# A 1024x1024 output product taken as seven products of quarters, with the weights' sums made by transfers in DRAM

## The chip, the cores and the metric

The kernel runs on one core of a Trainium2 chip. The metric is the device time of one execution in microseconds (us), as the median of several runs. The engines of the core are TensorE (PE, whose weight loads are listed apart as PEld), VectorE (DVE), ScalarE (ACT), GpSimd (POOL) and SyncE (SP), which here only issues transfers. Each engine takes its instructions from one queue in a fixed order.

## What is computed

Two transformer blocks on 512 tokens of width 1024, all in float32. The change lies in the end of the first block: the merged branches are multiplied by `w_out`.

```python
def first_block(x, p, ...):
    ...
    att_b = fox_branch(qb, kb, vb, log_f)                  # forgetting attention, 8 heads
    y_b = (att_b * silu(gate_b)) @ w_branch_b
    m_a, m_b = split(sigmoid(h @ w_merge))
    out = (m_a * y_a + m_b * y_b) @ w_out                  # [512, 1024] @ [1024, 1024]
    x = x + rmsnorm(out, g_post)
    e = p @ w_ple                                          # [512, 256] @ [256, 1024]
    gate = sigmoid(x @ w_ple_gate)
    x = x + rmsnorm(gate * e, g_ple)
    return x
```

The second block (attention, and a feed-forward part with `w_gate`, `w_up`, `w_down`) follows. The test compares with this reference in float32.

## The kernel before

Every float32 product is three matmuls: a value is split into a rounded part (`wh` of a weight, `ah` of an activation) and its rest (`wl`, `al`), and `wh*ah`, `wl*ah` and `wh*al` are added up in PSUM. A matmul here is 128x128 by 128x512.

Weights come as one stream. `specs` lists the products in the order of their use, `stream` cuts them into groups of 1024 columns (two 128-row chunks of 512 columns each, for the output product), and the stream is walked with a fixed lead: SP's queue loads a group into `raw` up to five groups ahead of use (`load_to`), and `convert_to` makes `wh` by a cast on ACT (L333) and `wl` by a subtraction on DVE (L334), up to three groups ahead. `wh` and `wl` have four buffers each, so the conversion of a group waits until the matmuls of the group four earlier are done. `send` hangs a further transfer behind the conversion of certain groups (`behind`). That is how sums of quarters of the second block's `w_down` come to DRAM: plain copies on SP's queue from the start of the stream on, and later adding transfers on POOL's queue (L249), each behind a one-element-per-partition copy `poke` (L248) that waits for that group's cast.

The feed-forward part at the end already takes `w_down` as a product of quarters with seven instead of eight products. The output product doesn't: it is `out0` and `out1`, two halves of the columns with eight chunks of the inner dimension each. Around it stand, in order of the program:

- the forgetting attention (`fox`), whose softmax scaling runs on POOL (L612 the reciprocal `rr`, L613 `P` times `rr`), whose transposes of `P` run on PE (L651), and into which products of later use are woven;
- `ya0` and `ya1`, whose results, per chunk of 128 columns, are evacuated by DVE (L986, L987) and split on ACT and DVE (L525) into `mh`, `ml`, the activation of the output product. This is transposed: columns on the partitions, tokens along the free dimension;
- the output product, with evacuation by `ev_out` (L1011 times `g_post`, L545 the square sum on ACT, L1014 the addition to `xr`, behind `rstd2` on POOL) and then `to_T`: eight transposes of the new `xr` of one token block on PE (L553), four to a PSUM bank `T`, of which there are two, each bank split into `x2h` (ACT, L521) and `x2l` (DVE, L522);
- `e0` and `e1`, the small product with `w_ple`, and then `pg0`, which reads `x2h` and `x2l`.

The order of these products on each engine is left to a scheduler, which mixes instructions of neighbouring products; inside `ordered()` the order on PE is that of the program instead. A list `late` holds back pieces of work for a number of steps (`LATE`), counted by `tick`.

## Time and profile before

| what | value |
|---|---|
| median of the runs | 1200.07 us (3 runs, 1199.03 to 1200.73) |
| the profiled execution's own time | 1198.17 us |
| its span, first to last instruction | 1196.4 us |
| mean granted clock of TensorE | 0.995 |
| busy: PE, DVE, ACT, POOL | 1166.9, 845.0, 637.9, 292.3 us |

The profile is of one execution. Busy time is the union of an engine's instructions. For PE the ends of matmuls are modelled, and they overlap: the pace of matmuls is read from their starts. An idle time stands in brackets behind an instruction, with the instruction that released it. The granted clock is a share of full speed, which is 2.4 GHz.

### The profile page before, as it was taken

How to read it: one execution, taken by the hardware profiler on the slowest of the kernel's cores; microseconds unless marked ns; L12 is line 12 of the kernel's file. 1: busy time of each engine (PE TensorE's matmuls, PEld its weight loads, DVE VectorE, ACT ScalarE, POOL GpSimd, SP SyncE). 2: the span in 40 equal slices, each digit the busy share in tenths (PEclk: the TensorE clock that was granted, in tenths of full speed). 3: DMA queues.
4: the chain of work that ended last, by engine and by line, in shares of the span. 5: the costliest groups of instructions: out<-in, count | busy, mean ns of one | idle time of the engine just before them, and what ended most of it. 6: DMA issues, size and time to landing. Idle time of an engine off the chain costs nothing.

```text
span 1196.4 us, 18475 instructions
## 1 busy us (share of the span) xinstructions
PE 1166.9 (98%) x6634; PEld 1009.8 (84%) x6634; DVE 845.0 (71%) x1569; ACT 637.9 (53%) x1260; POOL 292.3 (24%) x500
## 2 busy tenths in 40 slices
PE   7999999999999999999999999999999999999997
PEld 5898888888888888879888878888899999998885
DVE  5578767796565753776445478874698887877895
ACT  4466356535663444544466567752555455556564
POOL 2011065403341020211333435410022212200124
PEclk9999999999999999999999999999999999999999
DMA  5423613443223523324222222155369798857553
GB/s 195 102 92 119 191 48 119 126 137 102 95 71 106 181 85 109 127 90 128 57 71 72 72 60 79 60 158 193 124 127 185 147 190 151 141 132 268 170 184 114
DMA packets 117403, 148.89 MB, mean 124 GB/s; under 512 B 15552, under 2 KB 70080, under 8 KB 117312
## 3 DMA queue, kind: packets, MB, share of 16 engines
q1 hardware_dynamic: 94528, 136.18, 36.2%
q0 software_dynamic: 22784, 11.54, 8.2%
q8 instruction: 52, 0.85, 0.3%
q14 instruction: 39, 0.32, 0.1%
HBM read 141.40 MB, written 29.36 MB: 143 GB/s over the span
## 4 chain that ended last, share of the span: by engine, by line
PE 84%; DVE 4%; issue 4%; ACT 3%; POOL 2%; DMA 2%; SPq 0%; POOLq 0%; ACTq 0%; DVEq 0%
PE mm L422 49%; PE mm L1404 7%; PE E L1404 5%; PE R L1404 5%; PE S L1597 4%; PE AV L666 3%; PE E L1597 3%; PE T L651 2%; PE mm L1597 2%; DVE wl L334 1%; ACT wh L333 1%; DMA raw<-in_w_in_dram 1%; PE T L553 1%; PE S L885 1%; PE S L884 1%
## 5 line engine op out<-in xcount | busy, mean ns | idle before, releaser
L334 DVE TENSOR_TENSOR wl<-raw,wh 128x512 fp32r<-128x512 f32 (+4 forms) x219 | 203.2, 945 | 89.3 <-ACT wh L333 88.4
L333 ACT CAST wh<-raw 128x512 fp32r<-128x512 f32 (+4 forms) x219 | 173.7, 815 | 162.2 <-PE mm L422 65.7
L612 POOL TENSOR_TENSOR rr<-rs,mone 128x1 f32<-128x1 f32 x128 | 75.5, 590 | 166.5 <-ACT P L606 106.0
L522 DVE TENSOR_TENSOR pl<-T,ph 128x128 fp32r<-128x128 f32 (+3 forms) x152 | 61.9, 412 | 60.9 <-ACT ph L521 60.2
L422 PE MATMUL mm<-hh,wh 128*128 128x512 f32 x256 | 103.5, 405 | 0.0
L422 PE MATMUL mm<-hl,wh 128*128 128x512 f32 x256 | 101.4, 396 | 0.0
L422 PE MATMUL mm<-hh,wl 128*128 128x512 f32 x256 | 100.5, 395 | 0.0
L606 ACT ACTIVATE P<-P,nm 128x128 f32<-128x128 f32 (+2 forms) x96 | 51.5, 537 | 51.4 <-DVE nm L599 47.4
L521 ACT CAST ph<-T 128x128 fp32r<-128x128 f32 (+3 forms) x152 | 54.7, 362 | 43.5 <-PE T L651 32.1
L613 POOL TENSOR_SCALAR P<-P,rr 128x256 f32<-128x256 f32 (+3 forms) x128 | 73.4, 573 | 12.0
L333 ACT CAST wh<-qsum 128x1024 fp32r<-128x1024 f32 (+1 forms) x44 | 42.8, 974 | 53.9 <-PE R L1404 16.3
L1404 PE MATMUL R<-acts,wh 128*128 128x256 f32 x320 | 57.8, 281 | 0.0
L1404 PE MATMUL mm<-acts,wh 128*128 128x256 f32 x320 | 57.6, 280 | 0.0
L651 PE MATMUL T<-ident,P 128*128 128x128 f32 x296 | 54.3, 277 | 3.3 <-ACT km L1184 2.4
L422 PEld LDWEIGHTS mm<-hh,wl 128*128 128x128 f32 x256 | 48.0, 188 | 11.2
L1404 PE MATMUL E<-acts,wh 128*128 128x256 f32 x320 | 57.1, 280 | 0.0
L334 DVE TENSOR_TENSOR wl<-qsum,wh 128x1024 fp32r<-128x1024 f32 (+1 forms) x44 | 49.3, 1122 | 11.0 <-ACT wh L333 11.0
L422 PEld LDWEIGHTS mm<-hh,wh 128*128 128x128 f32 x256 | 48.2, 188 | 8.5
L422 PEld LDWEIGHTS mm<-hl,wh 128*128 128x128 f32 x256 | 48.2, 188 | 7.8
L422 PE MATMUL mm<-h2h,wh 128*128 128x512 f32 x128 | 53.6, 419 | 0.0
L422 PE MATMUL mm<-h2h,wl 128*128 128x512 f32 x128 | 50.6, 395 | 0.0
L422 PE MATMUL mm<-h2l,wh 128*128 128x512 f32 x128 | 50.1, 392 | 0.0
(431 smaller groups left out, 3458.8 us busy)
## 6 DMA issues: line engine op xcount, KB each, us to landing
raw<-in_w_in_dram SPq DMA_DIRECT2D x50, 512.0 KB, 3.7
down<-in_w_down_dram SPq DMA_DIRECT2D x16, 704.0 KB, 6.0
quart<-in_w_up_dram SPq DMA_DIRECT2D x20, 512.0 KB, 6.4
raw<-down SPq DMA_DIRECT2D x20, 512.0 KB, 3.9
raw<-in_w_merge_dram SPq DMA_DIRECT2D x16, 512.0 KB, 4.1
raw<-in_w_out_dram SPq DMA_DIRECT2D x16, 512.0 KB, 3.9
quart<-in_w_gate_dram SPq DMA_DIRECT2D x16, 512.0 KB, 5.2
raw<-in_w_down_dram SPq DMA_DIRECT2D x15, 512.0 KB, 4.3
```

The source lines that it names most:

```text
L333: mark_hi[0] = nc.scalar.copy(hi[:, js], raw[:, js]).ins
L334: mark[0] = nc.vector.tensor_sub(lo[:, js], raw[:, js], hi[:, js].bitcast(F32)).ins
L422: nc.tensor.matmul(o, x_, m, start=kc == 0 and k == 0 and n0 == 0, stop=last and k == 2)
L521: nc.scalar.copy(hi, src)
L522: nc.vector.tensor_sub(lo, src, hi.bitcast(F32))
L606: nc.scalar.activation(P[:, :n], P[:, :n], AF.Exp, bias=bias, scale=-1.0, accum_out=rs)
L612: nc.gpsimd.tensor_tensor(rr, rs, mone, op=OP.pow)
L613: nc.gpsimd.tensor_scalar(P[:, :n], P[:, :n], rr, 1.0, op0=OP.mult, op1=OP.mult)
L651: nc.tensor.transpose(T[:, i, :], P[:, blk(i)], ident)
L666: nc.tensor.matmul(self.av[:, q0:q0 + pc.stop - pc.start], self.v(kb), m, start=pi == 0 and i == 0, stop=pi == len(plan) - 1 and i == 1)
L1404: nc.tensor.matmul(R[:, c, :], w[:, kc, cs], m[:, kc, :], start=first and c + kc + k == 0, stop=kc == 3 and k == 2, skip_group_check=True)
L1597: nc.tensor.matmul(acc[b], a, w[:, j], start=first and kc == 0 and k == 0, stop=kc == 10 and k == 2, skip_group_check=True)
```

## The change

The output product is made by seven products of quarters (512x512) instead of the eight that two halves amount to: `A11`, `S4`, `A12`, `S2`, `S1`, `S3`, `A22`, each over 4 chunks of the inner dimension for 2 token blocks of 128 and 512 columns, with the three matmuls of the split. So the groups of the weight stream are 14 where they were 8, and everything behind them moves by that. Sums `S1` to `S4` of the weights' quarters are made in DRAM: four copies of 1 MB on SP's queue, behind the conversions of groups 14, 16, 18 and 20, and four adding transfers of 1 MB on POOL's queue behind the conversions of groups 27, 29, 31 and 35. The copies of `w_down`, which began at group 14, begin at 22; its adding transfers keep their places in the feed-forward part. The sums `T1` to `T4` of the activation's quarters are made in place in `ta` by DVE and split like the activation itself.

The results are put together from PSUM banks of three kinds: `S` for `A11`, `mm` and `AV` for `S4`, two `mm` for `U` (a negated copy of `A11` by ACT to which `S2` and `S3` add), and again `S` for `A22`. The whole from `A11` to `e1` stands in one `ordered()` block, and the transposes of `xr` wait eight steps (`LATE["out"]`). The transposes of `p` (`pst`) move ahead into `ya0` and `ya1`.

```diff
-    LATE = {"mla": 3, "pg1": 16, "q2": 8, "o21": 10}
+    LATE = {"mla": 3, "pg1": 16, "q2": 8, "o21": 10, "out": 8}
...
+    in_dram = {}
+    def quarter(base, w, name):
+        n = w.shape[0] // 2
+        if name[0] == "S":
+            if (base, name) not in in_dram:
+                in_dram[base, name] = tc.dram_tile([n, 512], F32, name=f"{base}{name}")
+            return in_dram[base, name]
+        r, c = n * (name[2] == "2"), 512 * (name[1] == "2")
+        return w[r:r + n, c:c + 512]
+    def quarters(base, w, order):
+        return {base + name: ([(quarter(base, w, name), 0, 512, 0)], w.shape[0] // 256) for name in order}
+    OUT = ("A11", "S4", "A12", "S2", "S1", "S3", "A22")
...
-        "out0": ([(w_out, 0, 512, 0)], 8),
-        "out1": ([(w_out, 512, 512, 0)], 8),
+        **quarters("out", w_out, OUT),
...
-        for some, engine, at, step in ((copies, nc.sync, 14, 2), (adds, nc.gpsimd, first_of["seven"], 4)):
+        def put(some, engine, base, w, rows, at):
             for dst, src in some:
-                for r in range(0, DFF // 2, 352):
-                    behind[at] = (engine, down_sums[dst][r:r + 352, :], down(src)[r:r + 352, :])
-                    at += step
+                for r in range(0, w.shape[0] // 2, rows):
+                    behind[at.pop(0)] = [engine] + [quarter(base, w, q)[r:r + rows, :] for q in (dst, src)]
+        put(copies, nc.sync, "out", w_out, 512, [14, 16, 18, 20])
+        put([adds[i] for i in (0, 3, 1, 2)], nc.gpsimd, "out", w_out, 512, [27, 29, 31, 35])
+        put(copies, nc.sync, "dn", w_down_2, 352, list(range(22, 54, 2)))
+        put(adds, nc.gpsimd, "dn", w_down_2, 352, list(range(first_of["seven"], first_of["seven"] + 64, 4)))
...
-    mh, ml = unit("mh", "U3"), unit("ml", "U6")
+    m21 = unit("m21", "U3", [128, 2, 4, 512])
+    m11 = unit("m11", "U6", [128, 2, 2, 4, 256])
+    mT = unit("mT", "U0", [128, 2, 2, 4, 256])
+    m4 = [pool.tile([128, 4, 256], FR, name="m4", tag=f"V{2 + k}") for k in range(2)]
+    mp = {"B11": m11[:, 0], "B22": m21[:, :, :, :256], "B21": m21[:, :, :, 256:], "T1": m11[:, 1],
+          "T2": mT[:, 0], "T3": mT[:, 1]}
+    mp = {**{n: [t[:, 0], t[:, 1]] for n, t in mp.items()}, "T4": m4}
     def ev_ya(g):
         def f(c, ps):
             i = 4 * g + c
             t = p2("ya")
             nc.vector.scalar_tensor_tensor(t, ta[:, i, :], 1.0, ps, op0=OP.add, op1=OP.mult)
-            nc.vector.tensor_add(t, t, acc[:, i, :])
-            split(mh[:, i, :], ml[:, i, :], t, 0.5)
+            m = ta[:, i, :]
+            nc.vector.tensor_add(m, t, acc[:, i, :])
+            if g == 0:
+                split(mp["B11"][0][:, c, :], mp["B11"][1][:, c, :], m[:, 256:], 0.5)
+            else:
+                split(m21[:, 0, c, :], m21[:, 1, c, :], m, 0.5)
         return f
...
-    ob = unit("ob", "U2", [128, NB, 1024], F32)
+    ob = unit("ob", "U4", [128, NB, 1024], F32)
     xr = unit("xr", "U5", [128, NB, 1024], F32)
     for tb in range(NB):
         nc.sync.dma_start(xr[:, tb, :], xv[:, tb, :])
     ssq = pool.tile([128, NB, 2], F32, name="ssq", tag="ssq")
-    x2h, x2l = unit("x2h", "U0"), unit("x2l", "U1")
-    pst = unit("pst", "U4", [128, NB, 256], F32)
+    pst = q4("pst", [128, NB, 256])
     nc.sync.dma_start(pst, p.rearrange("(b p) d -> p b d", p=128))
     pT = [pool.tile([128, 2, 512], FR, name="pT", tag=f"V{i}") for i in range(2)]
     for tb in range(NB):
         to_T(pst[:, tb, :], 2, pT[0], pT[1], tb)
     gb = g_bcast(g_post)
-    def ev_out(nh):
-        def f(tb, ps):
-            nc.vector.tensor_mul(ob[:, tb, 512 * nh:512 * nh + 512], ps, gb[:, 512 * nh:512 * nh + 512])
-            sum_sq(ps, ssq[:, tb, nh:nh + 1])
-            if nh == 1:
-                nc.vector.scalar_tensor_tensor(xr[:, tb, :], ob[:, tb, :], rstd2(ssq[:, tb, :], D), xr[:, tb, :],
-                                               op0=OP.mult, op1=OP.add)
-                to_T(xr[:, tb, :], 8, x2h, x2l, tb)
-        return f
-    run(product("out0", pair_act(mh, ml), ev_out(0), True))
-    run(product("out1", pair_act(mh, ml), ev_out(1), True, "tail"))
-    eb = unit("eb", "U4", [128, NB, 1024], F32)
+    x2 = []
+    def ev_out(nh, tb, ps):
+        nc.vector.tensor_mul(ob[:, tb, 512 * nh:512 * nh + 512], ps, gb[:, 512 * nh:512 * nh + 512])
+        sum_sq(ps, ssq[:, tb, nh:nh + 1], j=pool.tile([128, 512], F32, name="junk", tag="ph0"))
+        if nh == 1:
+            nc.vector.scalar_tensor_tensor(xr[:, tb, :], ob[:, tb, :], rstd2(ssq[:, tb, :], D), xr[:, tb, :],
+                                           op0=OP.mult, op1=OP.add)
+            if not x2:
+                x2.extend((unit("x2h", "U0"), unit("x2l", "U1")))
+            late.append([LATE["out"], lambda: to_T(xr[:, tb, :], 8, *x2, tb)])
...
+    ACT_OF = {"A11": "B11", "S4": "B22", "A12": "B21", "S1": "T1", "S2": "T2", "S3": "T3", "A22": "T4"}
+    def seven_tok(base, order, banks, pair, work, end):
+        R = {}
+        for n, name in enumerate(order):
+            into = {"A12": "A11", "S2": "U", "S3": "U", "S1": "S4"}.get(name, name)
+            if into not in R:
+                R[into] = [bank(k) for k in banks[into]]
+            f0 = first_of[base + name]
+            for i in range(8):
+                work(n, i)
+                kc, b = divmod(i, 2)
+                g, j = divmod(kc, 2)
+                convert_to(f0 + g)
+                wh, wl = ws[f0 + g]
+                ah, al = [t[:, kc, blk(b)] for t in pair[ACT_OF[name]]]
+                for k, (a, w) in enumerate(((ah, wh), (ah, wl), (al, wh))):
+                    nc.tensor.matmul(R[into][b], a, w[:, j], start=into == name and kc == 0 and k == 0,
+                                     stop=kc == 3 and k == 2, skip_group_check=True)
+                if i % 4 == 3:
+                    used(f0 + g)
+                yield 1.0
+                tick(1.0)
+            if name == "A11":
+                R["U"] = [bank(k) for k in banks["U"]]
+                for b in range(2):
+                    nc.scalar.activation(R["U"][b], R["A11"][b], AF.Copy, scale=-1.0)
+            end(name, R)
...
+    def out_work(n, i):
+        some = {(0, 4): lambda: (m_add("T1"), m_add("T3")), (1, 0): lambda: m_add("T2"),
+                (1, 4): lambda: m_part("T2", mp, 0.5), (2, 0): lambda: m_part("T1", mp, 0.5),
+                (2, 4): lambda: m_part("T3", mp, 0.5), (3, 0): lambda: m_add("T4"),
+                (3, 4): lambda: m_part("T4", mp, 0.5)}.get((n, i))
+        if some:
+            with tc.issue_after(mark[0]), tc.issue_after(mark_hi[0]):
+                some()
+    def out_end(name, R):
+        for b in range(2):
+            if name == "S4":
+                nc.scalar.copy(m_sub[b], R["S4"][b])
+            elif name == "A12":
+                ev_out(0, 2 + b, R["A11"][b])
+            elif name == "S2":
+                kept[b] = p2("u2")
+                nc.scalar.copy(kept[b], R["U"][b])
+            elif name == "S1":
+                c12 = p2("c12")
+                nc.vector.tensor_sub(c12, R["S4"][b], kept[b])
+                nc.vector.tensor_sub(m_sub[b], m_sub[b], R["S4"][b])
+                ev_out(0, b, c12)
+            elif name == "S3":
+                c22 = p2("c22")
+                nc.vector.tensor_add(c22, R["U"][b], m_sub[b])
+                kept[b] = p2("u3")
+                nc.scalar.copy(kept[b], R["U"][b])
+                ev_out(1, b, c22)
+            elif name == "A22":
+                nc.vector.tensor_add(kept[b], kept[b], R["A22"][b])
+                ev_out(1, 2 + b, kept[b])
+    eb = unit("eb", "U2", [128, NB, 1024], F32)
...
-    for nh in range(2):
-        run(product(f"e{nh}", lambda kc: (pT[0][:, kc, :], pT[1][:, kc, :]), ev_e(nh), True))
-    gs = unit("gs", "U2", [128, 4, 1024], F32)
+    with ordered():
+        for _ in itertools.chain(
+                seven_tok("out", OUT, {"A11": ("S", "S"), "S4": ("mm", "AV"), "U": ("mm", "mm"), "A22": ("S", "S")},
+                          mp, out_work, out_end),
+                *[product(f"e{nh}", lambda kc: (pT[0][:, kc, :], pT[1][:, kc, :]), ev_e(nh), True)
+                  for nh in range(2)]):
+            pass
```

The order of the instructions changes in three places. Names of the form `m_4093` are the activation's quarters and sums, `S`, `mm`, `AV`, `T` are PSUM banks; lines are those of the kernel before and of the changed kernel.

DVE between the evacuation of `ya1` and the start of the output product, before:

```order
L987 TENSOR_TENSOR ya<-ya,acc 128x512
L986 SCALAR_TENSOR_TENSOR ya<-ta,mm 128x512
L525 SCALAR_TENSOR_TENSOR ml<-ya,mh 128x512 x2
L987 TENSOR_TENSOR ya<-ya,acc 128x512
L525 SCALAR_TENSOR_TENSOR ml<-ya,mh 128x512
L986 SCALAR_TENSOR_TENSOR ya<-ta,mm 128x512
L334 TENSOR_TENSOR wl<-raw,wh 128x1024
L986 SCALAR_TENSOR_TENSOR ya<-ta,mm 128x512 x2
```

and the same place in the changed kernel:

```order
L1007 TENSOR_TENSOR ta<-ya,acc 128x512
L538 SCALAR_TENSOR_TENSOR m_4093<-ta,m_4093 128x256
L1005 SCALAR_TENSOR_TENSOR ya<-ta,mm 128x512
L538 SCALAR_TENSOR_TENSOR m_4093<-ta,m_4093 128x256 x2
L1007 TENSOR_TENSOR ta<-ya,acc 128x512
L1005 SCALAR_TENSOR_TENSOR ya<-ta,mm 128x512
L347 TENSOR_TENSOR wl<-raw,wh 128x1024
L1007 TENSOR_TENSOR ta<-ya,acc 128x512
L1005 SCALAR_TENSOR_TENSOR ya<-ta,mm 128x512
L538 SCALAR_TENSOR_TENSOR m_4092<-ta,m_4092 128x512
L1005 SCALAR_TENSOR_TENSOR ya<-ta,mm 128x512
```

The last row of each piece is the evacuation of `ya1`'s last chunk. The bank that it frees is now the second one of `A11`; before, the first matmuls of `out0` used other banks.

PE at the end of the output product, before:

```order
L422 MATMUL mm<-wh,mh 128x512
L422 MATMUL mm<-wl,mh 128x512
L422 MATMUL mm<-wh,ml 128x512
L553 MATMUL T<-ident,xr 128x128 x8
L422 MATMUL mm<-wh,pT 128x512
L422 MATMUL mm<-wl,pT 128x512
L422 MATMUL mm<-wh,pT 128x512 x2
L422 MATMUL mm<-wl,pT 128x512
```

and in the changed kernel:

```order
L1064 MATMUL S<-wh,m_4095 128x512
L1064 MATMUL S<-wl,m_4095 128x512
L1064 MATMUL S<-wh,m_4096 128x512
L566 MATMUL T<-ident,xr 128x128 x16
L435 MATMUL mm<-wh,pT 128x512
L435 MATMUL mm<-wl,pT 128x512
L435 MATMUL mm<-wh,pT 128x512 x2
L435 MATMUL mm<-wl,pT 128x512
```

The transposes of two token blocks now stand in one row of 16 ahead of `e0` (and those of the other two in a second row of 16 behind `e0`'s 24 matmuls), where four rows of eight stood among `e0`'s matmuls and ahead of them. DVE at the same place of the changed kernel, from the first `xr` to the second `x2l` and on to the third:

```order
L1036 SCALAR_TENSOR_TENSOR xr<-ob,rstd,xr 128x1024
L347 TENSOR_TENSOR wl<-raw,wh 128x1024
L1125 TENSOR_TENSOR u_4565<-u_4565,S 128x512
L1036 SCALAR_TENSOR_TENSOR xr<-ob,rstd,xr 128x1024
L1125 TENSOR_TENSOR u_4580<-u_4580,S 128x512
L347 TENSOR_TENSOR wl<-raw,wh 128x1024
L535 TENSOR_TENSOR x2l<-T,x2h 128x4x128
L1033 TENSOR_TENSOR ob<-u_4565,gb 128x512
L535 TENSOR_TENSOR x2l<-T,x2h 128x4x128
L1033 TENSOR_TENSOR ob<-u_4580,gb 128x512
L347 TENSOR_TENSOR wl<-raw,wh 128x1024
L1036 SCALAR_TENSOR_TENSOR xr<-ob,rstd,xr 128x1024
```

Before, the `x2l` of a token block stood in pairs with one `wl` or `xr` between the pairs.

POOL in the forgetting attention, before (`P<-P,rr` of 512 columns is the last key length of a head, of 128 the first of the next):

```order
L613 TENSOR_SCALAR P<-P,rr 128x512
L604 TENSOR_SCALAR bias<-nm,ctok 128x1
L612 TENSOR_TENSOR rr<-rs,mone 128x1
L604 TENSOR_SCALAR bias<-nm,ctok 128x1
L613 TENSOR_SCALAR P<-P,rr 128x128
L612 TENSOR_TENSOR rr<-rs,mone 128x1
```

and in the changed kernel:

```order
L617 TENSOR_SCALAR bias<-nm,ctok 128x1
L626 TENSOR_SCALAR P<-P,rr 128x512
L261 COPY poke<-wh 128x1
L262 DMA outS_82<-in_w_out_dram 512x4x128
L625 TENSOR_TENSOR rr<-rs,mone 128x1
L617 TENSOR_SCALAR bias<-nm,ctok 128x1
L626 TENSOR_SCALAR P<-P,rr 128x128
```

The copy and the adding transfer (`S3`) now stand ahead of the scaling of the next head's first block. The other one of this stage (`S1`) stands in the same way two blocks earlier, ahead of the scaling of 256 columns.

## Rows read from the trace of the kernel before

**Rows 1.** Busy time and share of the span by engine, from the page.

```profile
PE 1166.9 (98%) x6634; PEld 1009.8 (84%) x6634; DVE 845.0 (71%) x1569; ACT 637.9 (53%) x1260; POOL 292.3 (24%) x500
```

**Rows 2.** A stretch: us; PE, PEld, DVE, ACT, POOL busy; clock; DMA share; GB/s.

```profile
386.90:442.60 55.70, 55.70 (x245) 44.93 (x244) 33.84 (x46) 21.18 (x36) 4.90 (x9) 1.00 0.40 133
```

**Rows 3.** Timeline of PE in the output product: start, us, instruction.

```profile
396.90 0.39 PE L422 MATMUL mm<-wh,mh 128*128 128x512 f32 x1
...
420.12 0.40 PE L422 MATMUL mm<-wh,mh 128*128 128x512 f32 x1
...
420.82 0.40 PE L422 MATMUL mm<-wh,mh 128*128 128x512 f32 x1
```

**Rows 4.** Timeline of DVE from ya1's evacuation into the output product.

```profile
386.86 1.28 DVE L986 SCALAR_TENSOR_TENSOR ya<-ta,mm 128x512 f32<-128x512 f32 x2 [2.55 <-PE mm L422]
...
399.35 0.68 DVE L525 SCALAR_TENSOR_TENSOR ml<-ya,mh 128x512 fp32r<-128x512 f32 x1
...
404.95 0.76 DVE L522 TENSOR_TENSOR pT<-T,pT 128x256 fp32r<-128x256 f32 x2 [0.18 <-ACT pT L521]
```

**Rows 5.** Timeline of DVE at the output product's end.

```profile
436.86 1.29 DVE L1014 SCALAR_TENSOR_TENSOR xr<-ob,rstd,xr 128x1024 f32<-128x1024 f32 x1 [1.84 <-POOL rstd L540]
...
445.88 1.22 DVE L334 TENSOR_TENSOR wl<-raw,wh 128x1024 fp32r<-128x1024 f32 x1
447.02 1.28 DVE L522 TENSOR_TENSOR x2l<-T,x2h 128x512 fp32r<-128x512 f32 x2
```

**Rows 6.** Timeline of ACT at the output product's end.

```profile
435.05 0.60 ACT L545 ACTIVATE junk<-mm 128x512 f32<-128x512 f32 x1 [2.43 <-DVE ob L1011]
...
442.76 1.05 ACT L333 CAST wh<-raw 128x1024 fp32r<-128x1024 f32 x1 [0.39 <-PE mm L422]
```

**Rows 7.** w_down's adding transfers: ns of one (least/median/most), first and last start.

```profile
L249 POOL DMA_DIRECT2D down<-in_w_down_dram x8: 2126/2129/2402, 880.0 to 1043.0; - x8
L249 POOL DMA_DIRECT2D down<-down x8: 1473/1484/1512, 919.2 to 998.5; - x8
```

**Rows 8.** The copies ahead of them, same columns.

```profile
L248 POOL COPY poke<-wh x16: 183/1238/1287, 878.9 to 1042.7; 128x1 f32<-128x1 f32 x16
```

**Rows 9.** Timeline of PE in the forgetting attention: transposes of P.

```profile
187.57 0.40 PE L651 MATMUL T<-ident,P 128*128 128x128 f32 x2
...
189.55 0.49 PE L651 MATMUL T<-ident,P 128*128 128x128 f32 x3
...
193.61 0.66 PE L651 MATMUL T<-ident,P 128*128 128x128 f32 x4 [0.88 <-POOL P L613]
...
196.02 0.27 PE L651 MATMUL T<-ident,P 128*128 128x128 f32 x1
```

**Rows 10.** Timeline of POOL there: scaling of P.

```profile
184.44 0.48 POOL L613 TENSOR_SCALAR P<-P,rr 128x256 f32<-128x256 f32 x1
...
188.36 0.59 POOL L613 TENSOR_SCALAR P<-P,rr 128x384 f32<-128x384 f32 x1
...
195.43 0.37 POOL L613 TENSOR_SCALAR P<-P,rr 128x128 f32<-128x128 f32 x1
```

**Rows 11.** Timeline of PE: the instructions behind its two longest idle times here.

```profile
511.50 1.10 PE L553 MATMUL T<-ident,xn 128*128 128x128 f32 x8 [2.71 <-DVE xn L561]
...
695.50 0.44 PE L651 MATMUL T<-ident,P 128*128 128x128 f32 x2 [2.43 <-ACT km L1184]
```

**Rows 12.** Stretches behind the first of these, columns as in rows 2.

```profile
512.00:515.00 3.00, 3.00 (x13) 2.43 (x11) 2.20 (x4) 1.28 (x3) 1.17 (x2) 0.57 0.47 123
515.00:518.00 3.00, 3.00 (x13) 2.40 (x12) 1.25 (x4) 0.94 (x2) 0.74 (x2) 0.87 0.64 246
```

**Rows 13.** Transfers by kind, from the page: count, size, us to landing.

```profile
down<-in_w_down_dram SPq DMA_DIRECT2D x16, 704.0 KB, 6.0
```

**Rows 14.** Timeline of SP's queue: two of these copies that follow each other.

```profile
75.58 0.62 SPq L246 DMA_DIRECT2D down<-in_w_down_dram  x1
...
104.14 0.51 SPq L246 DMA_DIRECT2D down<-in_w_down_dram  x1
```

More of the change, by code (lines that the diff above doesn't have):

```diff
@@ new lines, in sums_of, with add, part @@
+    def sums_of(src):
+        at = {f"B{f}{t}": src[:, 4 * f - 4:4 * f, 512 - 256 * t:768 - 256 * t] for f in (1, 2) for t in (1, 2)}
+        T = {"T1": ("B11", "B11", OP.subtract, "B12"), "T3": ("B12", "B12", OP.subtract, "B22"),
+             "T2": ("B22", "B11", OP.add, "B22"), "T4": ("B21", "B21", OP.subtract, "B22")}
+        def add(name):
+            d, a, op, b = T[name]
+            nc.vector.tensor_tensor(at[d], at[a], at[b], op=op)
+        def part(name, pair, scale=None):
+            split(*pair[name], at[T[name][0]], scale)
+        return add, part
@@ L1058, in ev_pg @@
         return f
-    X2 = pair_act(x2h, x2l)
+    X2 = pair_act(*x2)
     run(product("pg0", X2, ev_pg(0), True, "head"))
@@ L1546, in dn_banks @@
     def dn_banks(kinds):
-        return [{"mm": mm_bank, "S": s_bank, "AV": av_bank,
-                 "T": lambda: t_bank("E").rearrange("p a b -> p (a b)")}[k]() for k in kinds]
+        return [bank(k) for k in kinds]
     def dn_end(name):
```

24 lines of the change are left out of this document (12 added, 12 removed).

## The prediction

> **What bounds the kernel now.** The busy table of the profile comes first: TensorE (PE) is busy for 1166.9 us, 98% of the span [rows 1]. So a removed matmul is worth its time only where nothing else becomes late. The table by stretches over the output product shows PE busy for every one of 55.70 us at full clock, with VectorE (DVE) busy for 33.84 us and ScalarE (ACT) for 21.18 us of them [rows 2]: inside this stage PE waits for nothing today, and what is saved there is saved at the matmul's own pace. That pace is read from starts, not from the recorded durations, which overlap: three matmuls of 128x512 take 0.70 us, from 420.12 to 420.82 [rows 3], so 0.233 us each.
>
> **Matmuls removed.** Before, 2 halves x 8 chunks of 128 x 4 tiles x 3 = 192. After, 7 products x 4 chunks x 2 token blocks x 3 = 168. 24 x 0.233 = **-5.6 us**. I see nothing else that gets shorter in this stage. The rest is waits.
>
> **The wait at A11.** The first new product writes two PSUM banks called S, and the second of them is free only when DVE has evacuated the last chunk of ya1. Before, the first output matmul starts at 396.90 [rows 3] while DVE is still evacuating, since it uses banks that are free earlier. How late is DVE? The first pair of ya1's evacuations starts at 386.86, the first split behind the last one at 399.35 [rows 4]. By the order 17 operations of 128x512 and two conversions (wl, 1.14 us each by the starts 445.88 and 447.02 [rows 5]) lie between, so one of the 17 takes (12.49 - 2.28)/17 = 0.60 us. After, by the new order, up to the operation that frees the bank there are 15 of these, two conversions, and six half-size ones at 0.34 us (a pair takes 0.76 us with its end [rows 4]): 9.0 + 2.3 + 2.0 = 13.3 us behind 386.86. PE gets there 10.04 us behind it (396.90), plus 0.4 us for eight transposes of p that now stand ahead, plus 0.7 us for the three matmuls into the first bank: 11.1 us. So **+2.2 us** (bounds 1.2, if three of the half-size ones are done in the 2.55 us that DVE idles ahead of 386.86, and 3.0, if ACT's casts ahead of the half-size ones hold DVE up).
>
> **The wait ahead of e0.** The order lets PE run the 16 transposes of token blocks 0 and 1 in one row right behind A22. They go through two PSUM banks of four, so the third four wait until DVE has written the first x2l, and the fourth for the second. Those two stand on DVE behind work of S3 and A22. I count from S3's last matmul. Four operations of 0.60 us (c22 and ob, twice), of which 0.5 lies ahead of it since the first bank ends earlier, end at 1.9. The square sum on ACT and the reciprocal root on POOL (1.81 us from 435.05 to 436.86, [rows 6, 5]) let the first xr (1.2 us) end at 3.9. Then come wl 5.0, A22's first sum 5.75 (its last matmul is at 5.6), the second xr 6.95, A22's second sum 7.55, wl 8.7, x2l 9.3, ob 9.9, x2l 10.5. With 0.1 us of signal and four transposes of 0.36 us, e0 starts at 10.95. Without a wait it would start at 5.6 + 1.6 = 7.2. So **+3.8 us** (bounds 2.7, when the two weight conversions on DVE slip behind, one of them 1.14, and 4.5). Before, the transposes stood in rows of eight with e0's matmuls between.
>
> **The wait behind e0.** The other 16 transposes stand behind e0's last matmul, and their x2l on DVE stand behind a conversion whose cast on ACT waits for that matmul. The cast starts about 0.3 us behind it (0.39 in its row) and takes 1.05 us [rows 6]; then 0.05, wl 1.14, two x2l of 0.60 [rows 5], 0.1 of signal and the last four transposes 0.36 make 4.2 us, where the transposes alone need 1.6. **+2.6 us** (2.3 to 3.0).
>
> **The adding transfers.** Four adds go from DRAM to DRAM on POOL's queue, and POOL's instruction writes the descriptors: 2.13 us for an add of w_down whose source is the input, 1.48 us for one between two sums, both of 1408 packets [rows 7]. An output quarter is 2048 packets, so an estimate in proportion is 3.1 us for a strided source. Ahead of each stands a one-column copy that waits for a weight cast (0.18 to 1.24 us [rows 8]; I take 0.4). Two of the four stand in the forgetting attention, where POOL's softmax scaling (P) feeds PE's transposes. The first stands ahead of the scaling that starts at 184.44 and lasts 0.48; its transposes are at 187.57, so 2.65 us of slack take the block but for a small rest that shows at the next head block (P from 188.36 for 0.59, transposes at 189.55, 0.60 of slack): +0.3. The second stands ahead of P at 195.43, which ends at 195.80, with the transpose at 196.02 [rows 9, 10]: 0.22 of slack against 0.4 + 2.13 to 3.1, so +2.5. Against them, the wait of 0.88 us for P at 193.61 [rows 9] goes: that chain leads back over an exponential on ACT that stood behind the cast of a weight group, and in the new order the cast stands behind it. 0.3 + 2.5 - 0.88 = **+1.9 us** (from -0.9, when neither add holds POOL, to +4.5, when both take the full 3.1 us and a 1.24 us copy and the wait stays). The other two adds lie where POOL has over 5 us of slack; without it each would cost some 2 us.
>
> The Trainium skill, DMA: Bandwidth & Descriptors, section "Anatomy of one DMA — SWDGE (gpsimd) path", says that descriptor generation is small and that many descriptors can be emitted before their cost shows, the fixed part being mostly the receipt at the end. The trace speaks against it here: the same 1408 packets hold POOL for 2.13 or 1.48 us by the source's shape [rows 7]. By the page the term would be -0.9 and the sum 2.8 us lower.
>
> **TensorE's clock.** Two idle times of PE in this trace, of 2.71 and of 2.43 us [rows 11], were followed by stretches at a lower granted clock: after the first, 0.57 of full speed over 3 us and 0.87 over the next 3 [rows 12], so a good 3 us at 1.2 GHz instead of 2.4, and 0.43 x 3 + 0.13 x 3 = 1.7 us lost. The 0.88 us at 193.61 was followed by none. The wait ahead of e0 comes in two pieces, of about 2 us each; the other three are estimated at 2.2 to 2.6. I take one drop and half of another: **+2.5 us** (0 to 5).
>
> **What I cost at nothing.** The new sums of activations, T1 to T4, and their splits: DVE has 22 us free of the 55.70 [rows 2], and A11's delay gives them more; if one were late it would cost the 1.2 us of a 128x1024 operation. The copies of quarters on SP: one of 704 KB lands in 6.0 us [rows 13], 1 MB by size in 8.7 and a weight load of 512 KB in 4.4; copies follow each other every 28.6 us (75.58 to 104.14 [rows 14]), in which two loads and a copy need 17.5. If that cover went, the next cast would be late by a copy's extra 2.7 us. The copies of w_down, moved later by eight groups, keep that spacing. The product's own weight groups are 14 instead of 8 and feed PE for only 12 x 0.233 = 2.8 us each. A load buffer is taken for a load, 4.4, and a conversion of 1.05 and 1.14 us, 6.6 in all; with three buffers (the third in `idx`) a group can come every 2.2 us. With two it would be 3.3, and PE would lose 0.5 x 14 = 7 us.
>
> **Sum.** -5.6 + 2.2 + 3.8 + 2.6 + 1.9 + 2.5 = +7.4 us. The profiled execution took 1198.2 us (span 1196.4 and 1.8 around it), so 1205.6 in its own terms; the median of the runs, 1200.07, lies 1.9 above it, so 1207.5, and I say **1207**.
>
> **The rivals.**
> *POOL is not held*: the descriptors are written beside the softmax. For it: the short record of 1.48 us [rows 7]. Against it: POOL's instructions stand in one queue, and the longer record. -5.6 + 8.6 - 0.9 and one clock drop, 1.7: +3.8, so 1203.9. Chance 0.12. This is what the page's rule above would make of it.
> *The waits of the output stage don't come* (8.6 us in three places). One mechanism would do it: DVE runs ahead of my count. It has 22 us free in the stage, and all three waits are lengths of its queue; if that is short when PE gets there, the banks S and T are free in time, and no clock falls behind these places. -5.6 + 1.9 = -3.7, so 1196.4. It decides when less than 1.3 us of the 8.6 are left: then the time is lower by over 0.2%, 2.4 us, about what a measurement of this kernel can tell from no change. Against it: each wait follows from a producer that the new order names, and DVE's pace is measured. Chance 0.12. With 1.3 to 6.1 us left the time is within 0.2%: chance 0.16.
> *Heavier*: the waits are each long enough that the clock falls behind all four, 4 x 1.7 = 6.8 instead of 2.5: +11.7, so 1211.8. For it: [rows 11, 12]. Against it: all four waits lie only about at the shortest that was followed by a drop, 2.43. Chance 0.10.
>
> **How the numbers follow.** My forecast, with all terms near their values (+2.4 to +11), has the remaining 0.50; with the first rival and the last, slower holds 0.72, the same 0.16, faster 0.12. The lower end, 1198.5, is a little below what the lower bounds give (-5.6 + 1.2 + 2.7 + 2.3 - 0.9 + 0 = -0.3, so 1199.8) and takes in most of the same; the upper, 1212.5, is just above the heavier rival. That leaves out the faster case and the far end of the upper bounds, some 2 in 10.
>
> **What would show it.** Right: PE records of 168 matmuls in the seven products, an idle time of some 2 us within the first six matmuls of A11, released by DVE's ya; two idle times inside the transposes behind A22, released by x2l, together near 4 us, and one of near 2.6 behind e0; a late P on POOL right behind the second adding transfer. Wrong: transposes behind A22 at an even pace, POOL's P on time, granted clock at 1.00 through the stage. The prediction would also be wrong if S1 to S4 were not in DRAM when their loads come, with PE waiting for a cast there.

## The result, and the profile after

The changed kernel takes 1212.89 us in the median (1211.82 to 1213.55, 4 runs), the kernel before, measured beside it, 1200.16 us: a ratio of 1.0106, with a 95% interval of 1.0089 to 1.0124. It is slower by 12.7 us where 7 were forecast, and 0.4 us above the range. The profiled execution took 1211.82 us, 13.65 more than the one before.

The table of waits of the changed kernel names for each pair of instruction and releaser the total, the number of times and the longest:

```profile
PE T L566 <- DVE x2l L535: 7.0, 2, 4.9
PE T L664 <- POOL P L626: 3.5, 3, 1.7
...
PE S L1064 <- DVE ya L1005: 2.3, 1, 2.3
```

All the waits that were forecast are there: x2l, P, ya. New and not forecast are waits for `nm` (1.1 us) and `aa` (0.7 us), which are in the sparse attention, long ahead of the output product. PE's timeline has them all in their places. First the transposes of P in the forgetting attention, which stood at 189.55, 193.61 and 196.02 [rows 9]:

```profile
190.66 0.55 PE L664 MATMUL T<-ident,P 128*128 128x128 f32 x3 [0.61 <-POOL P L626]
...
194.53 0.66 PE L664 MATMUL T<-ident,P 128*128 128x128 f32 x4 [1.17 <-POOL P L626]
...
198.79 0.33 PE L664 MATMUL T<-ident,P 128*128 128x128 f32 x1 [1.69 <-POOL P L626]
```

POOL's timeline shows what held P up, an add of 3.05 us and one of 2.85. The reciprocal behind each starts inside the add's record; it ends 3.67 and 3.46 us behind the add's start, where alone it takes 0.57. Ahead of the second P stands a `bias` of 1.35 us:

```profile
182.97 3.05 POOL L262 DMA_DIRECT2D outS<-in_w_out_dram  x1
184.78 1.86 POOL L625 TENSOR_TENSOR rr<-rs,mone 128x1 f32<-128x1 f32 x1
...
192.46 1.35 POOL L617 TENSOR_SCALAR bias<-nm,ctok 128x1 f32<-128x1 f32 x1
...
194.56 2.85 POOL L262 DMA_DIRECT2D outS<-in_w_out_dram  x1
196.19 1.83 POOL L625 TENSOR_TENSOR rr<-rs,mone 128x1 f32<-128x1 f32 x1
...
198.11 0.62 POOL L626 TENSOR_SCALAR P<-P,rr 128x128 f32<-128x128 f32 x1
```

Next the start of the sparse attention on PE, the kernel before (two scores, 2.41 us apart) and the changed kernel (the same two, 4.59 us apart):

```profile
277.82 0.22 PE L884 MATMUL S<-kik,qa 128*128 128x128 f32 x1
...
280.23 0.28 PE L884 MATMUL S<-kik,qa 128*128 128x256 f32 x1
```

```profile
280.64 0.22 PE L897 MATMUL S<-kik,qa 128*128 128x128 f32 x1
...
281.71 0.50 PE L435 MATMUL mm<-hh,wh 128*128 128x512 f32 x1 [0.74 <-DVE aa L889]
...
285.23 0.39 PE L897 MATMUL S<-kik,qa 128*128 128x256 f32 x1 [1.15 <-DVE nm L612]
```

Then PE in the output stage: A11's first matmul (396.90 before, [rows 3]), its second bank, A22's last matmul, and the two rows of 16 transposes:

```profile
403.00 0.40 PE L1064 MATMUL S<-wh,m 128*128 128x512 f32 x1
...
406.14 0.50 PE L1064 MATMUL S<-wh,m 128*128 128x512 f32 x1 [2.28 <-DVE ya L1005]
...
444.31 0.39 PE L1064 MATMUL S<-wh,m 128*128 128x512 f32 x1
445.28 1.07 PE L566 MATMUL T<-ident,xr 128*128 128x128 f32 x8 [0.58 <-DVE xr L1036]
451.27 2.32 PE L566 MATMUL T<-ident,xr 128*128 128x128 f32 x8 [4.92 <-DVE x2l L535]
...
463.47 1.25 PE L566 MATMUL T<-ident,xr 128*128 128x128 f32 x8 [2.13 <-DVE x2l L535]
```

The granted clock falls to its half level of 1.2 GHz during the long wait and is back some 7 us later, 5 of them with PE at work (stretches, columns as in [rows 2]; 0.62 over the third is half speed up to 456.3):

```profile
448.00:451.00 3.00, 0.00 (x0) 0.00 (x0) 3.00 (x4) 1.43 (x3) 2.82 (x3) 0.74 0.37 141
451.00:454.00 3.00, 2.65 (x10) 2.16 (x11) 3.00 (x5) 1.19 (x3) 2.15 (x4) 0.50 0.55 178
454.00:457.00 3.00, 3.00 (x10) 2.36 (x9) 3.00 (x4) 0.79 (x2) 0.00 (x0) 0.62 0.50 171
457.00:460.00 3.00, 3.00 (x14) 2.41 (x13) 0.74 (x2) 1.17 (x2) 0.00 (x0) 1.00 0.59 195
```

DVE's timeline across that wait says why it is 4.92 us and not less:

```profile
439.03 1.23 DVE L347 TENSOR_TENSOR wl<-raw,wh 128x1024 fp32r<-128x1024 f32 x1
440.17 0.69 DVE L1120 TENSOR_TENSOR c<-mm,sub 128x512 f32<-128x512 f32 x1
...
443.85 1.28 DVE L1036 SCALAR_TENSOR_TENSOR xr<-ob,rstd,xr 128x1024 f32<-128x1024 f32 x1 [0.93 <-POOL rstd L553]
...
447.59 1.28 DVE L1036 SCALAR_TENSOR_TENSOR xr<-ob,rstd,xr 128x1024 f32<-128x1024 f32 x1 [0.73 <-POOL rstd L553]
...
449.39 1.22 DVE L347 TENSOR_TENSOR wl<-raw,wh 128x1024 fp32r<-128x1024 f32 x1
450.53 0.68 DVE L535 TENSOR_TENSOR x2l<-T,x2h 128x512 fp32r<-128x512 f32 x1
...
451.73 0.68 DVE L535 TENSOR_TENSOR x2l<-T,x2h 128x512 fp32r<-128x512 f32 x1
```

A22's first matmul starts at 438.94, and S3's last is done about there. Only 1.2 us later, at 440.17, does DVE come to the first sum of S3's bank: it is still at S1's last `ob` and a conversion. Twice it waits for POOL's root besides, the second time since POOL had taken up operations of a later stage:

```profile
445.25 1.17 POOL L1182 TENSOR_SCALAR_AFFINE_SELECT bk<-bk 128x128 f32<-128x128 f32 x1
446.38 0.29 POOL L1184 TENSOR_SCALAR_AFFINE_SELECT bk<-bk 128x128 f32<-128x128 f32 x1
...
447.01 0.55 POOL L553 TENSOR_TENSOR rstd<-var,mhalf 128x1 f32<-128x1 f32 x1
```

### The profile page after: what moved, and what is told of

The parts are those of the page before. It is cut to its first block, busy times and chain, and to the rows that moved or that the text cites. A ratio compares the mean times of both kernels' runs of the same rounds, so it can differ in the third digit from the quotient of the medians.

```text
span 1210.1 us, 18507 instructions
## 1 busy us (share of the span) xinstructions
PE 1166.2 (96%) x6610; PEld 1007.8 (83%) x6610; DVE 865.7 (72%) x1591; ACT 651.3 (54%) x1278; POOL 307.7 (25%) x508
## 4 chain that ended last, share of the span: by engine, by line
PE 76%; DVE 9%; issue 5%; ACT 4%; POOL 3%; DMA 2%; SPq 0%; POOLq 0%; ACTq 0%; DVEq 0%
PE mm L435 41%; PE mm L1515 7%; PE E L1515 5%; PE R L1515 5%; PE S L1706 4%; PE E L1706 3%; DVE wl L347 2%; PE AV L679 2%; PE T L664 2%; PE mm L1706 2%; DMA raw<-in_w_in_dram 2%; ACT wh L346 1%; DVE mk L927 1%; POOL rr L625 1%; PE S L897 1%
## 5 line engine op out<-in xcount | busy, mean ns | idle before, releaser
L347 DVE TENSOR_TENSOR wl<-raw,wh 128x512 fp32r<-128x512 f32 (+3 forms) x225 | 210.8, 954 | 94.9 <-ACT wh L346 93.8
L346 ACT CAST wh<-raw 128x512 fp32r<-128x512 f32 (+3 forms) x225 | 179.9, 821 | 155.9 <-PE mm L435 59.8
L261 POOL COPY poke<-wh 128x1 f32<-128x1 f32 x20 | 15.9, 796 | 152.7 <-ACT wh L346 152.7
```

The lines of the kernel that those rows point to most:

```text
L346: mark_hi[0] = nc.scalar.copy(hi[:, js], raw[:, js]).ins
L347: mark[0] = nc.vector.tensor_sub(lo[:, js], raw[:, js], hi[:, js].bitcast(F32)).ins
```

## The experiments

The theory after the result: four separate causes, each with its place on PE's path. (1) POOL's queue is held by adding transfers; (2) with the adds where they stand, the scheduler orders DVE otherwise in the sparse attention; (3) x2l's place in DVE's queue lies behind the place of the transposes on PE, and the clock falls in that wait; (4) A11's bank. Rivals: the traffic of the transfers to memory is what costs, or DVE is overloaded throughout, so that a wait taken away comes back elsewhere. Times are medians; the kernel before was measured beside them each time, at 1198.9 to 1200.8 us, and a difference is to that one. A trace is of one execution.

**The adds moved to the end of the forgetting attention and behind it.**

```diff
-        ... nc.gpsimd, "out", w_out, 512, [27, 29, 31, 35])
+        ... nc.gpsimd, "out", w_out, 512, [31, 33, 35, 37])
```

> The changed kernel with its four adding transfers behind conversions 31, 33, 35, 37 instead of 27, 29, 31, 35. All four then stand on POOL behind the last scaling of the forgetting attention or where POOL has slack; the order on DVE in the sparse attention that follows stays as in the changed kernel. Theory (POOL is held by descriptor writing, and the loss of 2.2 us at the start of the sparse attention comes from the order on DVE): the late P goes, some 2.4 us less than the changed kernel, and the loss of 2.2 us in the sparse attention stays: about 1210.5. Rival (the transfers' traffic to memory slows the neighbours wherever it runs): no gain in sum, 1212 to 1213.

1211.95 us (ratio 1.0091, 1.0077 to 1.0104), 11.1 above before instead of 12.7. The 1.6 us between them are less than the two intervals can tell apart, so the median decides nothing between the theory and the rival; the trace does. In it PE waits 0.9 us for P in all, as before the change, and the waits for `aa` and `nm` (0.79 and 1.15 us) stay. Cause (1) and the place of (2) are as the theory has them.

**The adds at 35 to 41.**

> The same with the adds behind conversions 35, 37, 39, 41. The scheduler then leaves DVE's order in the sparse attention as it was before the change, but for one operation. Theory (DVE's order made the loss at the start of the sparse attention): the late P goes and the 2.2 us there go too, so 4 to 5 us less than the changed kernel, about 1208.3, and 2 us less than with the adds at 31. Rival (traffic of the transfers made that loss, since DVE and the weight loads meet it there): no better than with the adds at 31, about 1210.5 or more.

1215.99 us (1.0124, 1.0110 to 1.0138), worse. The waits for `aa` and `nm` are gone, but PE waits once for 4.9 us for P: the fourth add, which takes the sum that the third made, stands on POOL until that one has landed, and the sparse attention's first P behind it. POOL's timeline:

```profile
271.80 1.84 POOL L262 DMA_DIRECT2D outS<-outS  x1 [0.33 <-issue]
...
289.13 1.83 POOL L262 DMA_DIRECT2D outS<-outS  x1 [5.42 <-DMA outS<-outS]
```

Neither theory had this: an add holds POOL by its wait for another's landing, here 17 us from issue, more than by its own 1.84 us.

**All transposes 16 steps late instead of 8.**

```diff
-    LATE = {..., "out": 8}
+    LATE = {..., "out": 16}
```

> The changed kernel with LATE['out'] = 16 instead of 8: the transposes of token blocks 0 and 1 stand on PE behind e0's 24 matmuls, those of blocks 2 and 3 behind e1's. Theory (DVE reaches x2l late only because it is queued behind S3's and A22's results; 5.6 us of matmuls in between cover that): the waits of 5.9 and 2.3 us shrink to some 1 us each, which the two PSUM banks force, and the clock drop of 2.5 us does not come: 7 to 9 us less, about 1205. Rival (DVE is overloaded in the stage as a whole): the wait moves to the first matmuls of pg0, which need x2l, and less than 3 us are won, 1210 or more.

1210.12 us (1.0078, 1.0064 to 1.0092), 9.3 above before: some 3 us won, as the rival said, but not by its cause. The scheduler had put x2l behind the xr of token blocks 2 and 3 on DVE, so the wait only changed its place, with 5.6 us of matmuls ahead of it. DVE, then PE:

```profile
455.82 1.28 DVE L1036 SCALAR_TENSOR_TENSOR xr<-ob,rstd,xr 128x1024 f32<-128x1024 f32 x1 [0.72 <-POOL rstd L553]
457.02 1.28 DVE L535 TENSOR_TENSOR x2l<-T,x2h 128x512 fp32r<-128x512 f32 x2
```

```profile
457.76 0.48 PE L566 MATMUL T<-ident,xr 128*128 128x128 f32 x1 [5.55 <-DVE x2l L535]
```

**A11 in other banks.**

```diff
-                seven_tok("out", OUT, {"A11": ("S", "S"), "S4": ("mm", "AV"), ...
+                seven_tok("out", OUT, {"A11": ("mm", "AV"), "S4": ("S", "S"), ...
```

> The changed kernel with A11 in the banks mm and AV, and S4 in the two banks S, so that A11 no longer waits for the bank of ya1's last chunk. Theory (the wait of 2.4 us is that bank alone): it goes, about 2.4 us less, 1210.5. Rival (DVE's backlog behind ya1 is what counts, S4 reads halves of the same splits and its bank S comes free at the same time): the wait moves to S4's start and less than 1 us is won, 1212 or more.

1212.83 us (1.0102, 1.0088 to 1.0116): nothing won in the median. A11 no longer waits, and S4's splits come 1.12 us late instead:

```profile
415.40 0.74 PE L1064 MATMUL S<-wh,m 128*128 128x512 f32 x2 [1.12 <-DVE m L538]
```

**No sums in DRAM.** S1 to S4 of `w_out` are read as A21, A11, A11 and A12 of the input, and the eight transfers are left out.

> The changed kernel without the eight transfers for the sums of w_out's quarters: the four products that take a sum of weights take a plain quarter in its place (so the output product is another one). By the order, DVE's queue up to the output stage is then as before the change. Theory (the losses in the forgetting and at the start of the sparse attention, 2.4 and 2.2 us, both come with the adding transfers): both go, 4.6 us less, about 1208.3, and the waits of the output stage stay. Rival (the later copies of w_down, or the 14 weight groups, make them): no less than 1211.

1210.41 us (1.0090, 1.0076 to 1.0104). In the trace the matmuls from the second start of the sparse attention to its end lie less than 0.7 us later against the kernel before than those at the program's start: both losses are gone. The median is 11.6 above before and not 8.1. The clock is the likely reason: in the profiled execution it fell three times in the output stage (0.55 over 403 to 406 us, 0.50 over 450 to 453, 0.56 over 461 to 464), in the changed kernel's once, and its mean over the span is 0.988 to 0.991 in the four executions, where the changed kernel has 0.992. For the median the run is therefore no clean proof; the trace is.

**The transfers early**: copies behind conversions 3, 5, 7, 9 and adds behind 10, 11, 12, 13.

> The changed kernel with the copies behind conversions 3, 5, 7, 9 and the adds behind 10 to 13, ahead of the forgetting attention, where POOL has little to do; DVE's order from the first attention's second half on is that of the kernel before. Theory: both losses go, as without the transfers, 1208.3, and the traffic of the transfers costs nothing. Rival (their traffic costs time wherever they stand, 12 MB read and written beside the first weight loads): 1 to 4 us more than without them.

1219.67 us (1.0169, 1.0152 to 1.0187), 20.8 above before: slower than even the rival had it. There is one wait more, of the running sum of the forgetting attention's gates. It starts with an operation on POOL (L835, at 91.18) that stands behind the fourth add, and this add waits on POOL until the sum that it takes has landed:

```profile
PE C L840 <- DVE lf L837: 7.6, 1, 7.6
```

```profile
90.13 1.83 POOL L262 DMA_DIRECT2D outS<-outS  x1 [11.50 <-DMA outS<-outS]
```

Without the losses of 2.4 and 2.2 us and with this wait some 16 us would be left; the rest of the 20.8 was not followed up. The clock is part of it (mean 0.987 in the profiled execution).

**The transposes spread.**

```diff
-            late.append([LATE["out"], lambda: to_T(xr[:, tb, :], 8, *x2, tb)])
+            late.append([LATE["out"] + (0, 8, 4, 8)[tb], lambda: to_T(xr[:, tb, :], 8, *x2, tb)])
```

> The changed kernel with the transposes of the token blocks spread: block 0 behind A22, block 1 behind e0, block 2 in the middle of e1, block 3 behind e1. The first x2l stands on DVE where it stands in the changed kernel, not behind xr of blocks 2 and 3 as with all of them 16 steps late. Theory (the wait is the place of x2l in DVE's queue against the place of the transposes on PE): 0.7 us ahead of block 0's transposes, under 2 us for the rest, no clock drop: some 8 us less than the changed kernel, about 1205, and better than all 16 steps late by 5. Rival (DVE is overloaded from S3 on, some 20 us of work for 20 us of PE): a wait of 4 us or more stays, 1208 to 1210.

1205.07 us (1.0052, 1.0038 to 1.0066), 6.2 above before: 6.5 us won. The waits left are short, and the clock stays at 1.00:

```profile
446.35 1.07 PE L566 MATMUL T<-ident,xr 128*128 128x128 f32 x8 [0.56 <-DVE xr L1036]
...
458.27 0.66 PE L566 MATMUL T<-ident,xr 128*128 128x128 f32 x4 [1.26 <-DVE x2l L535]
...
460.01 0.66 PE L566 MATMUL T<-ident,xr 128*128 128x128 f32 x4 [1.08 <-DVE x2l L535]
```

Together with the early transfers (on record: about 1200 us if the two places add up, 1203 or more if they share a cause) it took 1211.37 us (1.0101, 1.0087 to 1.0114). It is over 1203, but for the wait of the run before, which is there with 6.8 us. Against that run the spread won 8.3 us, against the changed kernel 6.5, so the places are separate.

**The adds ahead of the forgetting attention**: copies behind 10, 12, 14, 16, adds behind 19, 21, 23, 25.

> The changed kernel with the copies behind conversions 10 to 16 (even) and the adds behind 19, 21, 23 and 25. In the order all four adds then stand on POOL between its casts of the keys and its first operation of the forgetting attention, a stretch in which the kernel before gives POOL nothing to do for 40 us; DVE's order in the sparse attention is that of before. Theory (what costs is POOL's queue standing behind an add while something waits for it, and the change of DVE's order; the traffic costs nothing): both losses go, 4 us less in the trace up to the output stage than the changed kernel, 8 to 9 us above the kernel before in the median. Rival (traffic, or an add's wait for the sum before it, costs time here too): 11 us or more above it.

1227.20 us (1.0236, 1.0220 to 1.0252), far off. The add's wait for the sum before it again, and longer (POOL's timeline; the attention's first operation on POOL, `bias`, stands behind it, and PE waits 13.8 us for P):

```profile
150.82 1.85 POOL L262 DMA_DIRECT2D outS<-outS  x1 [4.01 <-DMA outS<-in_w_out_dram]
...
170.92 1.83 POOL L262 DMA_DIRECT2D outS<-outS  x1 [13.17 <-DMA outS<-outS]
```

**The same with the transposes at offsets (2, 8, 6, 8)**, and **with p's transposes moved** from ya1 into the third and fourth product.

> The same, and the transposes of the token blocks spread: block 0 two steps into e0, block 1 behind e0, block 2 six steps into e1, block 3 at its end; the scheduler then mixes those of blocks 2 and 3 with the first products of pg0. Theory (places on PE against places on DVE): ahead of and behind e0 under 1 us of wait is left, no clock drop, so that only A11's 2.4 us stand against the 5.6 us of matmuls: 1 to 3 us faster than the kernel before. Rival (DVE is overloaded from S3 on): 2 to 4 us of wait stay at pg0, and the time is that of before or above.

> The same, and p's transposes moved from ya1 into the third and fourth product, which takes four operations of 0.34 us on DVE (1.4 us) from ahead of the operation that frees A11's second bank. Theory (A11's wait is DVE's queue, of which these are part): the wait falls from 2.4 to 1.1 us or so, 1.3 us less than without this edit, 3 us faster than the kernel before. Rival (ACT's halves or the weights' casts set DVE's pace there): no gain.

1218.17 us (1.0159) and 1218.00 us (1.0156). Both carry the loss of the run before, so their sums with the kernel before say nothing; against it the spread won 9 us. Moving p's transposes won nothing: the wait at A11 stayed at 2.3 us, since PE and DVE both get there earlier by what they no longer do.

**The adds at 33, 35, 37, 39**, where POOL has nothing to do for 40 us and no add waits into the attention behind.

> The changed kernel with the adds behind conversions 33, 35, 37 and 39. In the traces so far these conversions come at about 237, 246, 258 and 271 us, and POOL has nothing else to do from 241 to 281; an add that takes a sum made by another add waits some 18 us for that one to land, which here ends by 278, before the sparse attention's first operation on POOL. DVE's order is that of before but for one operation. Theory (an add costs time only where POOL's queue or DVE's order stands in the way): the 2.4 us of the forgetting attention and the 2.2 us at the start of the sparse attention are both gone, offset 0.5 to 1 us up to the output stage, 8 to 9 us above the kernel before in the median. Rival (the sums in DRAM cost time wherever they are made): 11 us or more above.

1208.86 us (1.0076, 1.0062 to 1.0090), 9.2 above before. The two scores of the sparse attention stand 2.43 us apart again, with no wait between them:

```profile
280.53 0.22 PE L897 MATMUL S<-kik,qa 128*128 128x128 f32 x1
...
282.96 0.28 PE L897 MATMUL S<-kik,qa 128*128 128x256 f32 x1
```

PE's waits for P are 0.9 us as before. So the transfers' traffic is not the cause of these two losses, with all 8 MB of it present.

**The same with the transposes spread**, at offsets (2, 8, 6, 8).

> The same with the transposes spread as in the run with the adds ahead of the forgetting attention (which gained 2.4 us over the output stage, from offset 22.0 to 19.6). If the places add up: 1 to 2.5 us faster than the kernel before. If the transfers or DVE's load leave another 2 us: the time of before.

1199.01 us, a ratio of 0.9997 (0.9987 to 1.0006): the time of the kernel before. Of the waits of the stage A11's is left, and here the clock falls behind it, which it didn't in the changed kernel:

```profile
403.69 0.50 PE L1064 MATMUL S<-wh,m 128*128 128x512 f32 x1 [2.28 <-DVE ya L1005]
```

```profile
404.00:407.00 3.00, 3.00 (x11) 2.37 (x10) 3.00 (x5) 1.02 (x2) 0.00 (x0) 0.70 0.39 111
407.00:410.00 3.00, 3.00 (x11) 2.37 (x10) 2.66 (x4) 1.44 (x3) 0.00 (x0) 0.73 0.87 249
```

**And A11 in the banks mm and AV, without and with p's transposes moved.**

> The kernel with the adds at 33 to 39 and the transposes spread (0.9997 of the kernel before), and A11 in the banks mm and AV. In its trace A11's wait of 2.4 us was followed by eight matmuls at half the pace, 0.43 us instead of 0.23, some 1.6 us. In the earlier run with these banks a wait of 1.3 us was left at S4 and no drop behind it. Theory (the wait at A11 and the drop behind it are what is left): 2.5 us less, about 1196.5, 0.2% below the kernel before. Rival (DVE's backlog then holds the products behind): the time of the kernel before.

> The same, with p's transposes moved from ya1 into the third and fourth product: four operations of 0.34 us less on DVE ahead of the splits that S4 waits for. Theory (S4's wait of 1.3 us is DVE's queue): it goes, 1196 or just under. Rival (ACT or the casts set the pace there, as the same edit left A11's wait at 2.3 us): no gain over the run before.

1198.52 us, 0.9992 (0.9982 to 1.0002), and 1200.91 us, 1.0006 (0.9996 to 1.0017). The wait at S4 is 1.1 us in both. Neither can be told from the kernel before: seven products in place of eight win at most 0.2% here. That doesn't mean that the stage wins nothing. In the profiled execution of the first of these, PE goes from the sparse attention's last product at 383.39 to the transposes of `xn` at 512.70 in 129.31 us, the kernel before from 379.64 to 511.50 [rows 11] in 131.86: 2.6 us less, of the 5.6 of the matmuls removed, with 1.1 us of wait left at S4 and 1.1 for x2l. But PE is 3.75 us behind when it gets there. It waited 9.7 us instead of 8.0 at the program's start (8.3 to 9.9 in the changed versions), and behind a wait of 0.87 us for P, which the kernel before has too, the clock fell:

```profile
196.00:199.00 3.00, 3.00 (x12) 2.62 (x12) 1.79 (x6) 1.57 (x5) 1.98 (x5) 0.57 0.85 302
```

So the rival that DVE is overloaded throughout, and each wait only moves, holds for A11's (to S4, 1.1 us of 2.3) but not for those of x2l. How much of the 2.6 us a median would show is open.

## Why the prediction was too low

By its own terms, with what the trace after has for each:

| term | predicted | measured |
|---|---|---|
| 24 matmuls fewer | -5.6 | -5.6 |
| wait at A11 | +2.2 | +2.3 |
| wait ahead of e0 | +3.8 | +5.5 (0.58 and 4.92) |
| wait behind e0 | +2.6 | +2.1 |
| adds in the forgetting attention | +1.9 | +2.6 (3.5 for P, less 0.9) |
| clock | +2.5 | +2.5 (half of 451.3 to 456.3) |
| sparse attention | 0 | +2.2 (4.59 less 2.41) |
| sum | +7.4 | +11.6 |

The profiled executions differ by 13.65, some 2 us more. Most of that is one more fall of the clock, late in the program. It follows waits of PE of 0.87 and 0.73 us; the kernel before has the same two (0.86 and 0.72), and its clock stays. The changed kernel, then the kernel before:

```profile
1091.00:1094.00 3.00, 3.00 (x18) 3.00 (x17) 2.23 (x4) 1.05 (x1) 0.00 (x0) 0.53 0.41 99
```

```profile
1078.00:1081.00 3.00, 3.00 (x26) 2.96 (x25) 2.81 (x6) 1.38 (x2) 0.00 (x0) 1.00 0.49 118
```

With 0.90 over the next 3 us it costs some 1.7 us, an estimate, and no edit stands there: of the 17 kernels profiled, the clock fell there in nine.

- **The matmuls**: A11's first starts at 403.00, A22's last at 444.31. That is 41.3 us for 168 matmuls, of which 167 x 0.233 = 38.9 and the wait at A11 2.3.
- **The wait at A11** is right in place, releaser and size: the count of DVE's operations holds. That its removal wins little was not foreseen: DVE's backlog holds S4 next.
- **The step that failed most** is "What I cost at nothing". It looked there for work that might be late, and at the adds only for what stands behind them on POOL. It did not look at the order on DVE, nearly 100 us behind the first add (182.97 to 280.6), where the scheduler now places a round of the top-k search (L926, L927) and the evacuations of `aa` otherwise. The section on the change names three places where the order changes; this is a fourth. DVE is busy without a break there, so the order decides what PE gets late: 2.2 us. In the order of DVE the search's rounds (MAX, MATCH_REPLACE) stand between the evacuations like this, before and then in the changed kernel:

```
L876 SCALAR_TENSOR_TENSOR aa<-th,mm 128x512 x2
L914 MATCH_REPLACE mk<-m_2782,mk 128x512
L876 SCALAR_TENSOR_TENSOR aa<-th,mm 128x512
L599 ISA P,nm<-S,causal 128x128
```

```
L889 SCALAR_TENSOR_TENSOR aa<-th,mm 128x512
L926 MAX m_2767<-mk 128x8
L604 SCALAR_TENSOR_TENSOR qa<-T,qa 64x4x128
L889 SCALAR_TENSOR_TENSOR aa<-th,mm 128x512
L927 MATCH_REPLACE mk<-m_2767,mk 128x512
L889 SCALAR_TENSOR_TENSOR aa<-th,mm 128x512
L612 ISA P,nm<-S,causal 128x128
```

  The first `aa` now comes right behind a conversion (`wl`, 279.84 to 280.98), and the second and third `aa` and the `nm` behind them stand behind a further MAX and qa. The run with the adds at 33 has the old order, the same transfers and none of this wait; the run with the adds at 31 has the new order and all of it. In all 17 traces the two go together: the new order and both waits in five kernels (adds from 27 or 31 on), the old order and neither wait in twelve.
- **The wait ahead of e0** had the right mechanism and the wrong size: it let DVE start on S3's sums 0.5 us ahead of S3's last matmul, and counted the square sum and "the reciprocal root on POOL" as 1.81 us. DVE started 1.2 us behind it, and from a square sum's start on ACT to its `xr` on DVE it took 2.47 us (441.38 to 443.85) and 4.18 (443.41 to 447.59), so that DVE idled for POOL's root twice (0.93 and 0.73 us), the second time behind `bk`. The first of the two pieces, 0.58, is a wait for `xr` and not, as forecast, for x2l. The upper bound given, 4.5, was too low by 1.
- **The adding transfers**: the estimate of 3.1 us in proportion to the packets was right (3.05 and 2.85). The first add's rest at the next head block, put at 0.3, was 0.61; the second add's wait, put at 2.5, was 1.69. But the wait of 0.88 us that was to go is still there, at 1.17: its `rr` did come earlier (191.89, before 192.19), but in POOL's new order, as printed in the section on the change, a `bias` stands between it and P, and took 1.35 us. The forecast that the other two cost nothing is right for their places in the changed kernel. What it left out is that an add waits on POOL for the landing of the sum that it takes, which there was over.
- **The clock**: one long drop at the wait ahead of e0, as large as the "one drop and half of another" that was put down; that the sizes agree is luck. None at A11 or behind e0.
- **The rivals**: "POOL is not held" falls, the Trainium skill's rule with it (DMA: Bandwidth & Descriptors, "Anatomy of one DMA — SWDGE (gpsimd) path"): the 2048 packets held POOL for 2.85 to 3.05 us with a strided source and 1.95 us between two sums. "The waits don't come" falls. "Heavier" was near in its time, 1211.8, but its cause, four clock drops, is not what happened.

Shown by runs: the holds on POOL, the place of x2l against that of the transposes, and that the two early losses are not the transfers' traffic. That it is the order on DVE which makes the loss in the sparse attention rests on versions that differ in it (the adds at 27 and at 31 have the waits, those at 33 and at 35 not, all with the same transfers); the order alone was not changed by itself.

## What to carry to other kernels

Where a scheduler sets the order, an instruction put on an idle engine can change the order on a full one far behind it: compare the whole order of the full engines, not only what stands around the edit. A product that saved 5.6 us of matmuls on the engine that bounds this kernel, by adding work to another, was paid back here in waits for that one; count that engine's queue from where it really stands when the stage begins, not from the event that you watch. A chain of adding transfers belongs where its queue has nothing behind it for the landing of each link, 14 to 20 us for 1 MB here, not only for the time of the add itself.

## What was not expected of the hardware

An adding transfer of 1 MB from DRAM to DRAM took about 17 us from issue to landing (271.80 to the release of the add that takes its sum, at 289.13, in the run with the adds at 35; 14.2 in the run with the early transfers, 20.1 in the one with the adds ahead of the attention), where the plain copies of 1 MB on SP's queue land in 6.9 in the changed kernel.

And the same wait of 2.28 us at A11, released by the same instruction, was followed by a fall of the granted clock in some versions (0.70 and 0.73 over the next 6 us in the run above) and by none in others. The changed kernel, right behind that wait:

```profile
407.00:410.00 3.00, 3.00 (x15) 2.40 (x14) 2.90 (x6) 1.57 (x3) 0.00 (x0) 1.00 0.52 163
```

Of the 13 profiled kernels that have this wait the clock fell in six. The length of a wait alone did not tell whether the clock falls, and with one profiled execution each, which of them had the fall may be chance. A difference of 1 to 2 us between two single executions can be no more than that.
